# A decoder layer in f32: the FFN input's weight sums go to VectorE, and the FFN output's loads and the gate product to GpSimd

## The chip, the cores and the metric

The kernel runs on one core of a Trainium2 chip. The time is the device time of one execution in microseconds, as the median of several runs. TensorE (PE) multiplies matrices, VectorE (DVE) and ScalarE (ACT) work element by element and read PSUM, GpSimd (POOL) works element by element on SBUF only, and SyncE (SP) issues DMAs. ACT and POOL can issue DMAs too. Each engine takes its instructions in order.

## The reference

One layer of 1024 tokens and width 1024 in f32. Its last third is what the change touches:

```python
def conv_glu(hn, w_ffn_in, conv_w, conv_b, w_ffn_out):
    a, gate = jnp.split(hn @ w_ffn_in, 2, axis=-1)        # 1024 x 5632, D_FF = 2816
    a_pad = jnp.pad(a, ((0, 0), (CONV_W - 1, 0), (0, 0)))
    conv = conv_b + sum(a_pad[:, j:j + S] * conv_w[j] for j in range(CONV_W))
    return (jax.nn.gelu(conv) * gate) @ w_ffn_out          # 2816 x 1024
```

Ahead of it stand a mixer of sparse and differential attention and a cross attention over 256 memory tokens, which the change does not touch.

## The kernel before, in words

Every f32 operand of a large product is split into a high and a low half, each in f32r: ScalarE copies the high half (`parts`, line 175), VectorE subtracts it from the source for the low half (line 178). A product is then three matmuls for each 128 rows of the contraction (`mm3`, lines 281 to 283). A split pair of weights of 128x512 is a page (`wp`, 12 of them).

The FFN input is computed in 22 tiles of 128 features (`ffn_in(f)`), each with seven products of 512 columns in place of eight, after Strassen and Winograd: sums of the four quarters of the operands are multiplied, and sums of the products give the four quarters of the result. The activations' sums are made once. The weights' sums are made for every tile: the tile's weights arrive in two raw tiles of 128x2x512, `a` and `g` (line 162, 512 KB each, on SP's queue), and four jobs work on them. Job A splits `a`'s two halves, B makes three sums (lines 199 to 201) and splits two of them, C makes a fourth sum (line 207) and splits two more operands, D splits the last. In tile 0 these sums run on VectorE, in the others on GpSimd. There are two raw tiles (`NRAW`), and `W.pump` splits the next job as soon as pages are counted free.

Each product has a PSUM bank; six banks turn. An add on VectorE (line 1427) or a copy on ScalarE (line 1432) takes it out into `p1`, `u2`, `v5` and the result's halves `a` and `g`. Behind the last add the tile's tail runs: ScalarE takes the first tap of the convolution (line 1468, ident), VectorE the other two (lines 1469, 1470), ScalarE the GELU (line 1471), VectorE multiplies by the gate (line 1472), and the result goes to `u_d` in HBM from ScalarE's queue (line 1473). The buffers of `a`, `g` and the convolution come from four `kq` tiles.

The FFN output has seven products as well, and its operands' sums are made ahead, in between: after each tile `fo_sums` takes a pair of rows of `w_ffn_out` (side w) or of `u_d` (side u), loads four tiles `fs` of 128x512 (line 1515, SP's queue, four buffers), and owes four steps, each a sum on GpSimd (line 1518) and its store to `ws_d` or `us_d` from GpSimd's queue (line 1519). `sums_step` makes one owed step where it is called. Then the FFN output itself runs: 77 steps, each with two loads of 256 KB on SP's queue (lines 1547, 1548), 14 steps ahead, a split over 128x1024 (lines 1556, 1557), and four products.

Up to the end of tile 0 TensorE's order is that of the program; all other orders, on every engine, are set by a planner that simulates the program and takes, on each engine, the first instruction in the program's order that its simulated time has ready. The order is then fixed.

The lines that the steps turn on:

```python
self.nsplit += 1
if len(self.raws) < NRAW - 1 or self.nload < self.nsplit:
    self.load()
```

Of the kernel before, what the change touches and what calls it, by code (L numbers as in the profile page):

```python
# [9 lines left out]
F32 = mybir.dt.float32  # L10
# [8 lines left out]
P = 128  # L19
# [5 lines left out]
FT = 22  # L25
# [19 lines left out]
def hybrid_layer(ctx, tc, I, out):  # L45
# [15 lines left out]
    def nm(s):  # L61
        cnt[0] += 1
        return f"{s}_{cnt[0]}"
# [68 lines left out]
    def wp():  # L132
        return wpool.tile([P, 2, 512], F32R, name=nm("wp"), tag="wp", bufs=NWP)

    def rawt():
        return wpool.tile([P, 2, 512], F32, name=nm("raw"), tag="raw", bufs=NRAW)

    class Weights:
# [41 lines left out]
        def split(self):  # L180
# [9 lines left out]
            if kind == "A":  # L190
                fi["a"] = raw
                fpart(raw[:, 0, :])
                fpart(raw[:, 1, :])
            elif kind == "B":
                fi["g"] = raw
                fi["s"] = s1 = page_s()
                a, g = fi["a"], raw
                eng = dve if key == ("fi", 0) else pool
                eng.tensor_tensor(s1, g[:, 0, :], g[:, 1, :], op=OP.add)  # L199
                eng.tensor_tensor(g[:, 0, :], a[:, 0, :], g[:, 0, :], op=OP.subtract)  # L200
                eng.tensor_tensor(a[:, 0, :], s1, a[:, 0, :], op=OP.subtract)  # L201
                fpart(a[:, 0, :])
                fpart(s1)
            elif kind == "C":
                a, g = fi["a"], fi["g"]
                eng = dve if key == ("fi", 0) else pool
                eng.tensor_tensor(a[:, 1, :], a[:, 1, :], a[:, 0, :], op=OP.subtract)
                fpart(g[:, 0, :])
                fpart(a[:, 1, :])
            elif kind == "D":  # L210
                fpart(fi["g"][:, 1, :])
            elif kind == "memT":
                for j in range(2):
                    pg = self.page(key)
                    for b in range(2):
                        v = slice(256 * b, 256 * b + 256)
                        gk = gmem[:, n + 2 * j + b:n + 2 * j + b + 1]
                        act.activation(pg[:, 0, v], raw[:, j, v], AF.Copy, scale=gk)
                        dve.scalar_tensor_tensor(pg[:, 1, v], raw[:, j, v], gk, pg[:, 0, v].bitcast(F32),
                                                 op0=OP.mult, op1=OP.subtract)  # L220
            elif kind == "xq":
                for j in range(2):
                    pg, gk = self.page(key), gxa[:, engines + j:engines + j + 1]
                    pool.tensor_scalar(pg[:, 0, :], raw[:, j, :], gk, 1.0, op0=OP.mult, op1=OP.mult)
                    dve.scalar_tensor_tensor(pg[:, 1, :], raw[:, j, :], gk, pg[:, 0, :].bitcast(F32), op0=OP.mult, op1=OP.subtract)
            else:
                for j in range(2):
                    self.parts(self.page(key), raw[:, j, :n], n, engines[j])
            self.nsplit += 1
            if len(self.raws) < NRAW - 1 or self.nload < self.nsplit:  # L230
                self.load()

        def pump(self, n=1):
# [923 lines left out]
        return w2_at[0].tile(shape, dt, name=nm(name), tag="w2", bufs=w2_at[1])  # L1157

    def fs():
        return w2_at[0].tile([P, 512], F32, name=nm("fs"), tag="fs", bufs=4)  # L1160

    def page_s():
        return pgp.tile([P, 512], F32, name=nm("ws"), tag="ws", bufs=1)
# [257 lines left out]
    def ffn_in(f):  # L1421
# [47 lines left out]
        dve.scalar_tensor_tensor(cv[:, 1:], a[:, :T - 1], cw[:, f, 1:2], cv[:, 1:], op0=OP.mult, op1=OP.add)  # L1469
        dve.scalar_tensor_tensor(cv[:, 2:], a[:, :T - 2], cw[:, f, 0:1], cv[:, 2:], op0=OP.mult, op1=OP.add)  # L1470
        act.activation(cv, cv, AF.Gelu_apprx_tanh)
        dve.tensor_tensor(g, cv, g, op=OP.mult)
        act.dma_start(u_d[f * P:(f + 1) * P, :], g)
        sums_step(4)
        if f % 2:
            owed_sums.extend(fo_sums("w", f // 2))
        elif f:
            owed_sums.extend(fo_sums("u", f // 2 - 1))
        if f == FT - 1:
            sums_step(4)  # L1480
            owed_sums.extend(fo_sums("u", f // 2))
            sums_step(4)

# [22 lines left out]
    def fo_sums(side, m):  # L1508

        src, d = (u_src, us_d) if side == "u" else (w_src, ws_d)  # L1510
        x = {}
        for odd in range(2):
            for half in range(2):
                x[odd, half] = fs()
                sp.dma_start(x[odd, half], src(m, odd, half))

        def one(j, o, p, q, op=OP.subtract):
            pool.tensor_tensor(o, p, q, op=op)  # L1518
            pool.dma_start(sum_at(d, j, m), o)
        x11, x21 = x[0, 0], (x[0, 1] if side == "u" else x[1, 0])  # L1520
        x12, x22 = (x[1, 0] if side == "u" else x[0, 1]), x[1, 1]
        if side == "u":
            return [lambda: one(0, x22, x21, x22, OP.add), lambda: one(2, x21, x11, x21),
                    lambda: one(1, x11, x22, x11), lambda: one(3, x12, x12, x11)]
        return [lambda: one(0, x11, x12, x11), lambda: one(2, x12, x22, x12),
                lambda: one(1, x22, x22, x11), lambda: one(3, x21, x21, x22)]

    owed_sums = []

# [43 lines left out]
            pass  # L1573

    w2_st.close()
    w2_at[:] = [ctx.enter_context(tc.tile_pool(name="w2q", bufs=1, reuse_waits="tile")), 5]
    for f in range(1, FT):
        for _ in ffn_in(f):
            pass
# [112 lines left out]
```

## Time and profile before

| what | value |
|---|---|
| median of 3 runs | 1758.92 us (1758.91 to 1760.85) |
| the profiled execution | 1757.62 us, span 1755.8 us |
| granted TensorE clock, mean | 0.957 |
| busy, PE / PEld / DVE / ACT / POOL | 91% / 74% / 73% / 42% / 38% |
| chain that ended last, by engine | PE 40%, DVE 31%, DMA 11%, issue 9%, POOL 5% |
| DMA | 220 MB, mean 125 GB/s |

A line of the page's groups reads: line, engine, operation, output<-input, count, then the busy time and the mean of one in ns, then the engine's idle time just before them and what ended it. Idle time is what an engine spends between instructions; a wait within an instruction shows as a longer duration. The granted clock is a share of 2.4 GHz; a stretch at 0.50 ran at 1.2 GHz.

### The profile page before, as it was taken

Reading aid. Unit: us, or ns where it says so; the run is one execution under the profiler, and the core shown is the slowest. Engines: PE = TensorE matmul, PEld = TensorE weight load, DVE = VectorE, ACT = ScalarE, POOL = GpSimd, SP = SyncE. Lnnn points to the kernel's source line nnn. Section 1 sums busy time; section 2 is a strip of 40 time slices with the busy share of each in tenths; the row PEclk is TensorE's granted clock in tenths of the full one; section 3 lists DMA queues with packets and bytes.
Section 4 is the critical chain, followed back from the end, with each engine's and each line's share of the span. In section 5 each row is a group of like instructions: output and inputs, shape, how many; then the busy total and the mean of one; then the engine's idle time right before and its main releaser. Section 6 shows DMA issues by size and latency. Waiting matters only on the chain.

```text
span 1755.8 us, 22643 instructions
## 1 busy us (share of the span) xinstructions
PE 1597.7 (91%) x7660; PEld 1303.6 (74%) x7660; DVE 1281.3 (73%) x2461; ACT 739.5 (42%) x1469; POOL 674.9 (38%) x862
## 2 busy tenths in 40 slices
PE   8899898788889999999999979998889889889999
PEld 7788676677777779877777757776667667668887
DVE  5746999998999894476453897777777777645564
ACT  6545576665664236144431343322222222333442
POOL 1647567356310230221010165654556655330111
PEclk9999989898999999999999989999999999889999
DMA  8222135222121221443030214444444444698811
GB/s 279 87 85 65 56 99 167 71 91 75 56 82 49 84 73 43 128 149 107 1 109 35 93 44 165 158 160 162 168 156 155 146 144 162 237 361 311 288 49 66
DMA packets 117795, 220.07 MB, mean 125 GB/s; under 512 B 18480, under 2 KB 38448, under 8 KB 117680
## 3 DMA queue, kind: packets, MB, share of 16 engines
q1 hardware_dynamic: 103744, 171.44, 29.8%
q0 software_dynamic: 8320, 27.27, 4.0%
q10 hardware_dynamic: 5616, 19.93, 2.9%
q8 instruction: 60, 0.98, 0.2%
q14 instruction: 55, 0.45, 0.1%
HBM read 160.92 MB, written 57.67 MB: 124 GB/s over the span
## 4 chain that ended last, share of the span: by engine, by line
PE 40%; DVE 31%; DMA 11%; issue 9%; POOL 5%; ACT 3%; SPq 0%; POOLq 0%; DVEq 0%; ACTq 0%
PE acc L281 7%; PE acc L282 7%; PE acc L283 7%; DVE jk L538 5%; DVE wp L178 5%; DMA raw<-in_w_ffn_in_dram 5%; PE big L281 2%; PE big L283 2%; PE big L282 2%; PE big L1249 2%; POOL raw L201 2%; DVE fc L1470 2%; PE acc L1010 1%; DVE ea L992 1%; DVE e L747 1%
## 5 line engine op out<-in xcount | busy, mean ns | idle before, releaser
L178 DVE TENSOR_TENSOR wp<-raw,wp 128x512 fp32r<-128x512 f32 (+1 forms) x200 | 214.4, 1087 | 97.6 <-ACT wp L175 89.7
L175 ACT CAST wp<-raw 128x512 fp32r<-128x512 f32 (+1 forms) x188 | 111.2, 616 | 221.9 <-DMA raw<-in_w_ffn_in_dram 94.3
L1557 DVE TENSOR_TENSOR wp<-fo,wp 128x1024 fp32r<-128x1024 f32 x77 | 99.9, 1312 | 95.5 <-ACT wp L1556 92.1
L1518 POOL TENSOR_TENSOR fs<-fs,fs 128x512 f32<-128x512 f32 x88 | 125.7, 1429 | 68.3 <-DMA fs<-in_w_ffn_out_dram 56.8
L1556 ACT CAST wp<-fo 128x1024 fp32r<-128x1024 f32 x77 | 79.7, 1049 | 128.3 <-PE big L283 47.3
L281 PE MATMUL acc<-wp,xh 128*128 128x512 f32 (+1 forms) x272 | 111.0, 411 | 8.7 <-ACT X L619 8.7
L177 POOL TENSOR_SCALAR wp<-raw 128x512 fp32r<-128x512 f32 (+1 forms) x64 | 45.3, 718 | 180.1 <-DVE rst L110 63.5
L282 PE MATMUL acc<-wp,xh 128*128 128x512 f32 (+1 forms) x272 | 110.4, 407 | 0.0
L283 PE MATMUL acc<-wp,xl 128*128 128x512 f32 (+1 forms) x272 | 110.2, 406 | 0.0
L655 ACT COPY pt<-trp 128x512 f32<-128x512 f32 (+3 forms) x144 | 65.6, 476 | 73.4 <-PE trp L664 72.9
L178 POOL TENSOR_TENSOR wp<-raw,wp 128x512 fp32r<-128x512 f32 x52 | 69.2, 1348 | 46.1 <-ACT wp L175 45.9
L199 POOL TENSOR_TENSOR ws<-raw 128x512 f32<-128x512 f32 x21 | 29.4, 1400 | 146.2 <-DMA raw<-in_w_ffn_in_dram 95.2
L1602 POOL TENSOR_TENSOR hr<-hr,r 128x512 f32<-128x512 f32 x16 | 26.8, 1688 | 152.1 <-DVE r L1618 78.6
L1010 PEld LDWEIGHTS acc<-va_t,pt 128*128 128x128 f32 x576 | 73.4, 193 | 6.4 <-ACT pt L655 4.3
L1010 PE MATMUL acc<-va_t,pt 128*128 128x65 f32 x576 | 75.8, 271 | 2.2 <-ACT pt L655 1.9
L1055 POOL DMA_DIRECT2D h_d<-xr x16 | 9.4, 586 | 167.0 <-DVE xr L1054 148.7
L993 ACT ACTIVATE ea<-ea,sta 128x128 f32<-128x128 f32 (+7 forms) x64 | 49.4, 777 | 51.4 <-DVE sta L992 47.9
L281 PEld LDWEIGHTS acc<-wp,xh 128*128 128x128 f32 x272 | 53.2, 196 | 21.9 <-ACT X L619 10.5
L538 DVE TENSOR_SCALAR_CACHE_REDUCE jk<-mb,cx 128x640 bf16<-128x640 uint16 (+1 forms) x64 | 68.6, 1072 | 0.7
L538 DVE TENSOR_SCALAR_CACHE_REDUCE jk<-mb,cand 128x640 bf16<-128x640 bf16 (+3 forms) x60 | 64.4, 1074 | 0.4
L282 PE MATMUL acc<-wp,wp 128*128 128x512 f32 x152 | 61.4, 404 | 3.5 <-DVE wp L178 3.0
L1469 DVE SCALAR_TENSOR_TENSOR fc<-fa,cw,fc 128x1023 f32<-128x1023 f32 x22 | 42.6, 1937 | 27.5 <-ACT fc L1468 27.5
(419 smaller groups left out, 5168.9 us busy)
## 6 DMA issues: line engine op xcount, KB each, us to landing
raw<-in_w_ffn_in_dram SPq DMA_DIRECT2D x44, 512.0 KB, 5.1
fs<-in_w_ffn_out_dram SPq DMA_DIRECT2D x44, 256.0 KB, 4.8
u_d<-fg ACTq DMA_DIRECT2D x22, 512.0 KB, 5.2
ws_d<-fs POOLq DMA_DIRECT2D x44, 256.0 KB, 2.7
fs<-u_d SPq DMA_DIRECT2D x44, 256.0 KB, 3.3
us_d<-fs POOLq DMA_DIRECT2D x44, 256.0 KB, 2.3
fo<-us_d SPq DMA_DIRECT2D x44, 256.0 KB, 5.3
fo<-ws_d SPq DMA_DIRECT2D x44, 256.0 KB, 5.4
```

Of the source, the lines that this page charges most:

```text
L175: act.copy(pg[:, 0, :n], src)
L178: (dve if el == "d" else pool).tensor_tensor(pg[:, 1, :n], src, pg[:, 0, :n].bitcast(F32), op=OP.subtract)
L281: pe.matmul(o, lhsT=lh, rhs=rh, start=start, stop=False)
L282: pe.matmul(o, lhsT=lh, rhs=rl, start=False, stop=False)
L283: pe.matmul(o, lhsT=ll, rhs=rh, start=False, stop=stop)
L538: dve.tensor_scalar(jk[:, :n], src, th[:, j:j + 1], None, op0=OP.is_ge, op1=OP.add, accum_out=cnt[:, j:j + 1])
L655: act.copy(dst, src)
L993: last["act"] = act.activation(e[:, :n], e[:, :n], AF.Exp, bias=st[:, 0, h:h + 1], scale=-1.0)
L1010: pe.matmul(acc[:, hh * 65:hh * 65 + 65], lhsT=pt, rhs=va_t[:, kt, :], start=kt == 0, stop=kt == i)
L1518: pool.tensor_tensor(o, p, q, op=op)
L1556: act.copy(hi, raw)
L1557: dve.tensor_tensor(lo, raw, hi.bitcast(F32), op=OP.subtract)
```

## The change

Seven things change. The four sums of a tile's weights run on VectorE in all tiles; the first three are made in job A, which now loads `g` itself if it is not there, the fourth in job B. From tile 1 on there is a third raw tile, taken by every third load, and loads run one further ahead. `w2` has four buffers in that stage instead of five, and `fs` three instead of four. The gate product and the store to `u_d` go to GpSimd and its queue, except in the last tile. The loads of `fo_sums` go to GpSimd's queue. They are no longer issued together when the sums become owed: a first owed step issues three, and the fourth follows the third sum, so five steps are owed for each side. `sums_step` is called once more in each tile, and with 5 instead of 4 at its end.

```diff
+    raw3 = []
     def rawt():
+        if raw3:
+            raw3[1] += 1
+            if raw3[1] % 3 == 0:
+                return raw3[0].tile([P, 2, 512], F32, name=nm("raw"), tag="raw3", bufs=1)
         return wpool.tile([P, 2, 512], F32, name=nm("raw"), tag="raw", bufs=NRAW)
...
             if kind == "A":
                 fi["a"] = raw
                 fpart(raw[:, 0, :])
                 fpart(raw[:, 1, :])
+                if i + 1 not in self.raws:
+                    self.load()
+                a, g = raw, self.raws[i + 1]
+                fi["s"] = s1 = page_s()
+                dve.tensor_tensor(s1, g[:, 0, :], g[:, 1, :], op=OP.add)
+                dve.tensor_tensor(g[:, 0, :], a[:, 0, :], g[:, 0, :], op=OP.subtract)
+                dve.tensor_tensor(a[:, 0, :], s1, a[:, 0, :], op=OP.subtract)
             elif kind == "B":
                 fi["g"] = raw
-                fi["s"] = s1 = page_s()
-                a, g = fi["a"], raw
-                eng = dve if key == ("fi", 0) else pool
-                eng.tensor_tensor(s1, g[:, 0, :], g[:, 1, :], op=OP.add)
-                eng.tensor_tensor(g[:, 0, :], a[:, 0, :], g[:, 0, :], op=OP.subtract)
-                eng.tensor_tensor(a[:, 0, :], s1, a[:, 0, :], op=OP.subtract)
+                a = fi["a"]
                 fpart(a[:, 0, :])
-                fpart(s1)
+                fpart(fi["s"])
+                dve.tensor_tensor(a[:, 1, :], a[:, 1, :], a[:, 0, :], op=OP.subtract)
             elif kind == "C":
-                a, g = fi["a"], fi["g"]
-                eng = dve if key == ("fi", 0) else pool
-                eng.tensor_tensor(a[:, 1, :], a[:, 1, :], a[:, 0, :], op=OP.subtract)
-                fpart(g[:, 0, :])
-                fpart(a[:, 1, :])
+                fpart(fi["g"][:, 0, :])
+                fpart(fi["a"][:, 1, :])
...
-            if len(self.raws) < NRAW - 1 or self.nload < self.nsplit:
+            if len(self.raws) < NRAW - 1 + len(raw3) // 2 or self.nload < self.nsplit:
...
-        return w2_at[0].tile([P, 512], F32, name=nm("fs"), tag="fs", bufs=4)
+        return w2_at[0].tile([P, 512], F32, name=nm("fs"), tag="fs", bufs=3)
...
-        dve.tensor_tensor(g, cv, g, op=OP.mult)
-        act.dma_start(u_d[f * P:(f + 1) * P, :], g)
-        sums_step(4)
+        if f == FT - 1:
+            dve.tensor_tensor(g, cv, g, op=OP.mult)
+            act.dma_start(u_d[f * P:(f + 1) * P, :], g)
+        else:
+            pool.tensor_tensor(g, cv, g, op=OP.mult)
+            pool.dma_start(u_d[f * P:(f + 1) * P, :], g)
+        sums_step(5)
...
-        x = {}
-        for odd in range(2):
-            for half in range(2):
-                x[odd, half] = fs()
-                sp.dma_start(x[odd, half], src(m, odd, half))
+        def ld(odd, half):
+            t = fs()
+            pool.dma_start(t, src(m, odd, half))
+            return t
...
+            def start():
+                x["22"], x["21"], x["11"] = ld(1, 1), ld(0, 1), ld(0, 0)
+
+            def third():
+                one(1, x["11"], x["22"], x["11"])
+                x["12"] = ld(1, 0)
+            return [start, lambda: one(0, x["22"], x["21"], x["22"], OP.add), lambda: one(2, x["21"], x["11"], x["21"]),
+                    third, lambda: one(3, x["12"], x["12"], x["11"])]
...
-    w2_at[:] = [ctx.enter_context(tc.tile_pool(name="w2q", bufs=1, reuse_waits="tile")), 5]
+    w2_at[:] = [ctx.enter_context(tc.tile_pool(name="w2q", bufs=1, reuse_waits="tile")), 4]
+    raw3[:] = [w2_at[0], 0]
```

Side w of `fo_sums` is changed in the same way as side u, shown here.

## Rows read from the trace of the kernel before

**Rows 1.** The page: busy us (share of the span) xinstructions of each engine.

```profile
PE 1597.7 (91%) x7660; PEld 1303.6 (74%) x7660; DVE 1281.3 (73%) x2461; ACT 739.5 (42%) x1469; POOL 674.9 (38%) x862
```

**Rows 2.** Windows: length, busy us (instructions) by engine, granted clock, DMA share, GB/s.

```profile
1083.00:1524.00 441.00, 394.54 (x1597) 311.02 (x1596) 326.37 (x311) 123.60 (x183) 254.38 (x226) 0.95 0.46 156
1524.00:1570.00 46.00, 33.81 (x125) 26.25 (x124) 24.45 (x25) 17.09 (x18) 6.91 (x7) 0.81 1.01 375
1570.00:1752.00 182.00, 181.81 (x803) 150.20 (x801) 98.77 (x90) 67.78 (x69) 34.28 (x24) 1.00 0.53 189
```

**Rows 3.** TensorE's timeline: start us, duration us, line, operation, output<-input, idle and releaser.

```profile
1290.80 0.40 PE L281 MATMUL acc<-B,wp 128*128 128x512 f32 x1
...
1293.60 0.40 PE L281 MATMUL trp<-T,wp 128*128 128x512 f32 x1
...
1330.38 0.76 PE L281 MATMUL acc<-B,wp 128*128 128x512 f32 x1 [3.83 <-DVE fg L1427]
```

**Rows 4.** TensorE's waits, 1083 to 1524: us in total, times, longest; six rows.

```profile
PE trp L281 <- DVE fg L1427: 12.7, 3, 4.3
...
PE big L281 <- DVE u L1427: 1.4, 1, 1.4
```

**Rows 5.** Window right behind a long wait of TensorE.

```profile
1330.00:1335.00 5.00, 4.62 (x11) 3.68 (x12) 5.00 (x6) 1.57 (x2) 1.79 (x2) 0.50 0.45 161
```

**Rows 6.** Chain of waits, 1311 to 1337: start us, us, what.

```profile
1312.86 5.02 DMA raw<-in_w_ffn_in_dram
...
1324.27 0.63 ACT wp L175
...
1329.56 0.68 DVE fg L1427
...
1332.98 1.22 DVE wp L178 x2
...
1334.22 4.79 DMA raw<-in_w_ffn_in_dram
```

**Rows 7.** VectorE's timeline in that stretch.

```profile
1324.92 4.71 DVE L178 TENSOR_TENSOR wp<-raw,wp 128x512 fp32r<-128x512 f32 x1 [1.84 <-ACT wp L175]
```

**Rows 8.** GpSimd's timeline in that stretch.

```profile
1324.76 1.31 POOL L1518 TENSOR_TENSOR fs<-fs,fs 128x512 f32<-128x512 f32 x1
...
1327.80 1.27 POOL L1518 TENSOR_TENSOR fs<-fs,fs 128x512 f32<-128x512 f32 x1
1329.37 0.56 POOL L1519 DMA_DIRECT2D us_d<-fs  x1 [0.30 <-POOL fs L1518]
```

**Rows 9.** VectorE by line, 1083 to 1524: count, busy us, mean ns, idle before, releaser.

```profile
L178 DVE TENSOR_TENSOR wp<-raw,wp 128x512 fp32r<-128x512 f32 x106 | 138.8, 1322 | 78.1 <-ACT wp L175 78.1
L1469 DVE SCALAR_TENSOR_TENSOR fc<-fa,cw,fc 128x1023 f32<-128x1023 f32 x19 | 37.9, 1993 | 26.1 <-ACT fc L1468 26.1
```

**Rows 10.** SP's queue's waits, 1083 to 1524.

```profile
SPq L162 <- DVE wp L178: 107.5, 34, 7.0
SPq L1515 <- POOL fs L1518: 107.1, 19, 10.7
```

**Rows 11.** Window of the instructions on raw tiles: VectorE, ScalarE, GpSimd busy.

```profile
1083.00:1524.00 441.00, 138.81 (x106) 63.29 (x106) 105.58 (x72) 0.95 0.46 156
```

**Rows 12.** GpSimd by line, whole span: a 128x1024 tensor_tensor.

```profile
L1174 POOL TENSOR_TENSOR kxl<-kxr,kxh 128x1024 fp32r<-128x1024 f32 x2 | 4.8, 2403 | 0.2
```

**Rows 13.** DMA issues, 1083 to 1524: count, size, median us to landing.

```profile
fs<-in_w_ffn_out_dram SPq DMA_DIRECT2D x38, 256.0 KB, 4.3
u_d<-fg ACTq DMA_DIRECT2D x19, 512.0 KB, 5.2
```

**Rows 14.** GpSimd's DMA issues to us_d: ns min/median/max.

```profile
L1519 POOL DMA_DIRECT2D us_d<-fs x40: 557/557/559, 1089.6 to 1517.5; - x40
```

**Rows 15.** TensorE's waits, 1524 to the end.

```profile
PE acc L281 <- ACT wp L1556: 7.4, 1, 7.4
PE acc L281 <- DVE v L1427: 4.2, 1, 4.2
```

More of the change, by code (lines that the diff above doesn't have):

```diff
@@ L1478, in ffn_in @@
             owed_sums.extend(fo_sums("u", f // 2 - 1))
+        sums_step()
         if f == FT - 1:
-            sums_step(4)
+            sums_step(5)
             owed_sums.extend(fo_sums("u", f // 2))
-            sums_step(4)
+            sums_step(5)
     NM = FT // 2
@@ L1519, in one, with start, third @@
             pool.dma_start(sum_at(d, j, m), o)
-        x11, x21 = x[0, 0], (x[0, 1] if side == "u" else x[1, 0])
-        x12, x22 = (x[1, 0] if side == "u" else x[0, 1]), x[1, 1]
+        x = {}
         if side == "u":
[L1523 to L1526, printed above, removed]
+            def start():
[5 more added lines that the diff above has]
+                    third, lambda: one(3, x["12"], x["12"], x["11"])]
+        def start():
+            x["11"], x["12"], x["22"] = ld(0, 0), ld(0, 1), ld(1, 1)
+        def third():
+            one(1, x["22"], x["22"], x["11"])
+            x["21"] = ld(1, 0)
+        return [start, lambda: one(0, x["11"], x["12"], x["11"]), lambda: one(2, x["12"], x["22"], x["12"]),
+                third, lambda: one(3, x["21"], x["21"], x["22"])]
     owed_sums = []
```

## The prediction

> **What bounds the kernel now.** I read the page's busy shares first: TensorE is busy 91% of a span of 1755.8 us and no other engine over 73% [rows 1], so the question is where TensorE is not at full speed. The table of windows answers it by stage [rows 2]: the FFN input's steady part, 1083 to 1524 us, has TensorE busy 394.5 of 441 us at a granted clock of 0.95; the change of stage behind it, 46 us, only 33.8 at 0.81; and the FFN output that follows is full (181.8 of 182, clock 1.00). Nothing is to be won in the last.
>
> In the timeline of TensorE a product of 12 matmuls takes 2.80 us when it is fed (one begins at 1290.80, the next at 1293.60) [rows 3]. The 441 us hold 1596 matmuls, 19 tiles of 84, which at that pace is 133 x 2.80 = 372.4 us. So 68.6 us are lost, and a tile takes 23.2 us where 19.6 would do. TensorE's waits in the window stand in six rows from 12.7 down to 1.4 us, 46.3 us together [rows 4]. The other 22 us follow each long wait: behind the one that ends at 1330.38 the window 1330 to 1335 has a granted clock of 0.50, the 1.2 GHz level, against 1.00 in the FFN output [rows 2, 3, 5]. What removes a wait gives its 2 us or so of slow clock back too.
>
> All these waits name an add on VectorE (line 1427), which frees the PSUM bank that the product wants. The add is late, not slow (0.68 us). The chain of waits shows why, from 1312.86 on [rows 6]: a raw weight tile is loaded (5.02 us), GpSimd makes its sums (landed 1317.9, done 1324.2, with a sum of the FFN output between them), ScalarE makes the high half (0.63 at 1324.27), and then VectorE's low half starts at 1324.92 and lasts 4.71 us [rows 7], where a free operation of its shape, as the add, takes 0.68. The add of `fg` stands behind it, at 1329.56, and TensorE goes on at 1330.38. In GpSimd's timeline three tensor_tensors and a DMA issue fill those 4.1 us without a pause [rows 8]; VectorE gets in at the first gap, at 1329.07. The same picture (one split of about 4.7 us behind such a run) stands in most tiles: the 106 splits of this form average 1322 ns [rows 9]. Then the other splits free the raw tile, and only at 1334.22 does the next load start. With two raw tiles for two loads a tile, this ring (load, sums, splits, free) is the period: 21.4 us here, and SP's queue spends 107.5 us waiting for a split to free a raw tile [rows 10].
>
> **The change part by part.**
> *Sums to VectorE, at the job before.* GpSimd loses 4 tensor_tensors a tile, 72 in the window and 105.6 us [rows 11], 5.9 us a tile. VectorE gets them: no row shows this sum there, the nearest is the split (same shape, two inputs in SBUF): two of them begun within 1.22 us when nothing holds them [rows 6], 1.32 each on average as they are held now. I take 0.60, so 2.4 us a tile, the upper end being 5.3. In the ring the sums' 6.2 us become about 2.
>
> *Third raw tile.* The first load of a tile no longer waits for the tile before. The ring now spans three half-tile slots: load 5.0, sums 1.8, five casts (0.62) and splits (0.60) and 2 us of waits, so some 15 us, against the 29 us (1.5 x 19.6) that three slots allow. The load is then hidden; if it weren't, the 5 us would be back. The price in SBUF (one `w2` and one `fs` buffer less) I put at nothing: three `w2` tiles live per product tile, four remain, and the FFN output's residual tiles come four at a time.
>
> *Gate product to GpSimd.* VectorE loses a 128x1024 tensor_tensor (1.2 us, twice the 0.60). GpSimd gains one; the row of that shape there takes 2.40 us [rows 12]. It lies at the end of a tile's chain (ident, convolution, GELU, gate, store). Its result's buffer is wanted only when the next tile's convolution buffer is taken, one tile later. Counted from the last add: ident, two of convolution and GELU at no more than the 2.0 us that the slowest of them has on average [rows 9], 8 us, then 2.4 + 0.6 for gate and issue and a store of 5.2 [rows 13]: 16.2 us, under 19.6. Hidden as long as GpSimd gets to it within 3 us.
>
> *Loads to GpSimd's queue.* Four loads and the store of u are issued there, 0.557 us each [rows 14], 2.8 us a tile; SP loses the loads, which held it 107.1 us and more [rows 10]. Raw loads, and later the FFN output's, stand free behind them. GpSimd per tile: 4 x 1.30 + 2.40 + 9 x 0.557 + 4 pauses of 0.30 = 13.8 us, plus what it waits for loads.
>
> The Trainium skill (SBUF — State Buffer, Summary: rules for kernel authors) advises against DMAs from GpSimd beside VectorE, since descriptor generation is starved while VectorE runs a two-port mode. The 40 issues from there to us_d last 557 to 559 ns with VectorE busy 74% of the time [rows 2, 14], so nothing of it shows. If it held for these operations, the five new issues would each wait for one operation of 0.7 to 2 us.
>
> *VectorE's own time*, the new limit to look at: 7 splits, 7 adds at 0.60 and three passes of 1.2 are 12.0 us now; 12.0 + 2.4 - 1.2 = 13.2 after. It is busy 326.4 / 19 = 17.2 us a tile now [rows 2], so 5 to 6 us are waits behind GpSimd. GpSimd's reading operations fall from 8 x 1.3 = 10.4 to 5.2 + 2.4 = 7.6 us, and its sums now alternate with their own stores, with a pause after each, so the runs of 4 us go. In proportion 4.3 us of waits are left: 17.5, with the 1.4 us in which the convolution waits for ScalarE [rows 9] 18.9 of 19.6. That fits, barely. The same page (section "Who interferes with whom") has the loser wait for one instruction of the other; the row of 4.71 us shows a wait over three. By the page the wait would be smaller than mine.
>
> I therefore don't take TensorE's floor but a period of 20.7 us, 1.1 above it: about the share that the waits now have, scaled by GpSimd's smaller part, (23.2 - 19.6) x 4.3 / 5.5 x 0.4, where 0.4 is my estimate of how much of a wait still reaches TensorE once sums and load are off the ring. The gain is (23.2 - 20.7) x 19 = 48 us.
>
> *The change of stage.* TensorE waits 4.2 us for an add and 7.4 us for a cast there [rows 15]. The first loads of the FFN output stand in SP's queue behind fs loads, though the first of them needs only the pages that the last tile's first product frees, some 13 us before the tile's end; with SP free it can go earlier. The bounds are -14 us (both waits and their slow clock go) and +5 (one more landing exposed, as the 5.2 us of the store of u [rows 13]); I take -3, since the 7.4 us hang on the last tile's store, which stays on ScalarE's queue.
>
> Sum: the profiled execution took 1757.6 us; 1757.6 - 48 - 3 = 1706.6, and the median of the runs is 1.3 above it: 1708.
>
> **Rivals.**
> *GpSimd becomes the period.* It runs in order, and its loads now wait where its arithmetic is queued. If each tile is gate, store, three loads, three sums, load, sum, one after the other, both load times are exposed: 13.8 + 2 x 4.3 (the median landing of the loads of w [rows 13]) = 22.4 us. A late gate then holds the convolution buffer, ScalarE's in-order queue and its casts. Gain (23.2 - 22.4) x 19 = 15: about 1743. For it: one buffer fewer for these loads, and none is fetched ahead. Against: the second load's wait can be filled by the next gate. The skill's starvation rule would add five waits of 0.7, 3.5 us, and turn this into a loss.
>
> *VectorE becomes the period (slower).* If GpSimd's reads block it for their whole length, 13.2 + 7.6 + 1.4, and it still waits for casts as now (78.1 / 19 = 4.1 [rows 9]), a tile takes 26.3 us: 3.1 x 19 = 59 us more, about 1817. It decides from the point at which VectorE's waits pass 10.0 us a tile (13.2 + 10.0 = 23.2). The likelier small form is the sums themselves: they stand in VectorE's order ahead of adds and wait there for the load; with a whole load of 5.0 us exposed in each tile, VectorE's 18.9 become 23.9, 0.7 over the old period: 1772. Against: the second load of a tile starts when the fifth split is done, well ahead.
>
> *The stall only moves (no change).* The order of instructions is set by the planner's own clock; if splits still stand ahead of late operands, the period stays: 1759.
>
> **How the numbers follow.** Forecast (period 19.6 to about 21.9, and the bounds of the change of stage; 1676 to 1730): 0.57. GpSimd as period (1730 to 1755): 0.19. No change: 0.08. Slower: 0.16, mostly its small form. A difference under 0.2% (3.5 us) can't be told from none. Faster 0.76, same 0.08, slower 0.16. Most of the forecast's mass lies above the floor; the range is 1682 to 1754, which takes in the GpSimd case; the forecast's own range is 1682 to 1728.
>
> **What would show it.** Right: the splits' mean under 0.9 us, none of 4.7; GpSimd without lines 199 to 207; raw loads issued with no wait of a whole tile; TensorE's waits in the stage under 20 us and its clock at 0.98 or more. GpSimd's rival: gates that start 5 us or more after GELU ends, ScalarE waiting for the store of u. VectorE's: sums waiting for raw loads, VectorE busy over 90%. A prediction of 1708 is wrong if the tile's period stays above 22 us, or if the change of stage costs 5 us or more.

## The result, and the profile after

The changed kernel takes 1694.44 us (median of 4 runs, 1689.76 to 1697.69) against 1759.88 for the kernel before on the same chip: a ratio of 0.963, 95% interval 0.960 to 0.965. Predicted were 1708 us, in a range of 1682 to 1754. The profiled execution took 1697.69 us; all stage figures below are of profiled executions.

The page of the changed kernel: span, and busy us of each engine as in [rows 1].

```profile
span 1695.9 us, 22395 instructions
...
PE 1570.8 (93%) x7660; PEld 1284.2 (76%) x7660; DVE 1296.0 (76%) x2524; ACT 736.7 (43%) x1469; POOL 666.8 (39%) x908
```

TensorE has 27 us less busy time for the same 7660 matmuls: its clock was slow for less of the time. Windows of the changed kernel, columns as in [rows 2]. The first is the same 19 tiles (1596 matmuls, counted back from the FFN input's last one), the second the change of stage, the third the FFN output.

```profile
1081.89:1472.88 390.99, 376.98 (x1597) 298.49 (x1596) 343.07 (x370) 124.00 (x185) 241.60 (x260) 1.00 0.53 180
1472.88:1510.00 37.12, 30.26 (x124) 24.49 (x123) 18.88 (x14) 12.34 (x13) 18.20 (x20) 0.91 0.91 335
1510.00:1692.00 182.00, 181.84 (x803) 150.23 (x801) 97.34 (x90) 67.83 (x69) 38.87 (x30) 1.00 0.58 209
```

Counted the same way the stage before was 441.05 us, and what follows it to the end of the span 231.69; now they are 390.99 and 223.02 (1695.9 - 1472.88). So of the 59.9 us by which the span is shorter, 50.1 come from the stage (a period of 20.58 us instead of 23.21), 8.7 from behind it and 1.2 from ahead of it. The granted clock of the stage rose from 0.95 to 1.00.

TensorE's waits in the stage (us in total, times, longest), which answer to [rows 4]; three smaller rows between the third and the last are left out:

```profile
PE acc L287 <- DVE fa L1433: 3.9, 4, 1.5
PE big L287 <- DVE fa L1433: 3.7, 4, 1.4
PE trp L287 <- DVE fa L1433: 3.4, 3, 1.8
...
PE trp L287 <- DVE v L1433: 0.6, 1, 0.6
```

All seven rows together are 14.0 us where there were 46.3, and the longest wait is 1.8 us where it was 5.3. They still name VectorE's adds. VectorE's lines in the stage, as in [rows 9]: the high-low splits, both convolution passes, and the first of the weight sums that it now makes (count, busy us, mean ns, idle before and its releaser).

```profile
L184 DVE TENSOR_TENSOR wp<-raw,wp 128x512 fp32r<-128x512 f32 x106 | 118.2, 1115 | 4.9 <-ACT wp L181 4.9
L1476 DVE SCALAR_TENSOR_TENSOR fc<-fa,cw,fc 128x1022 f32<-128x1022 f32 x19 | 47.1, 2481 | 0.0
L1475 DVE SCALAR_TENSOR_TENSOR fc<-fa,cw,fc 128x1023 f32<-128x1023 f32 x19 | 31.7, 1668 | 12.6 <-ACT fc L1474 12.6
L204 DVE TENSOR_TENSOR ws<-raw 128x512 f32<-128x512 f32 x17 | 17.4, 1022 | 27.4 <-DMA raw<-in_w_ffn_in_dram 27.4
```

The second convolution pass had this line before the change:

```profile
L1470 DVE SCALAR_TENSOR_TENSOR fc<-fa,cw,fc 128x1022 f32<-128x1022 f32 x19 | 29.3, 1542 | 0.0
```

The splits fell from 1322 to 1115 ns, but that pass (now L1476) went from 1542 ns to 2481: VectorE is still held, by other instructions and at other places. Its timeline in one tile (start, duration, line), the two held ones:

```profile
1321.54 2.81 DVE L1476 SCALAR_TENSOR_TENSOR fc<-fa,cw,fc 128x1022 f32<-128x1022 f32 x1
...
1326.05 2.51 DVE L184 TENSOR_TENSOR wp<-raw,wp 128x512 fp32r<-128x512 f32 x1 [0.49 <-ACT wp L181]
```

and GpSimd's timeline beside it:

```profile
1321.95 1.31 POOL L1529 TENSOR_TENSOR fs<-fs,fs 128x512 f32<-128x512 f32 x1
...
1325.59 2.41 POOL L1482 TENSOR_TENSOR fg<-fc,fg 128x1024 f32<-128x1024 f32 x1 [0.93 <-ACT fc L1477]
1328.44 1.28 POOL L1529 TENSOR_TENSOR fs<-fs,fs 128x512 f32<-128x512 f32 x1 [0.43 <-DMA fs<-in_w_ffn_out_dram]
```

The pass overlaps one operand sum; the split starts half a us into the gate's product, which ends at 1328.00, and lasts until 1328.56: nearly the whole of a free split (0.68 us) comes behind the gate. Splits of 4.7 us beside runs of three GpSimd operations [rows 7, 8] are gone, the longest of the stage lasts 3.3 us; single operations, sums and the gate, still hold VectorE.

SP's queue in the stage, as in [rows 10]:

```profile
SPq L168 <- DVE wp L184: 340.7, 33, 20.1
```

Its wait for a free raw tile grew from 107.5 to 340.7 us. That is no new stall: until the FFN output's first loads the queue has nothing else to issue, stands ready, and waits for a free raw tile as it should.

Behind the stage TensorE has one wait, which takes the place of both in [rows 15]:

```profile
PE acc L287 <- DVE fg L1433: 6.9, 1, 6.9
```

How it comes about is read from three timelines around it: GpSimd,

```profile
1477.04 0.55 POOL L1525 DMA_DIRECT2D fs<-u_d  x1 [0.81 <-DMA us_d<-fs]
1479.24 0.55 POOL L1525 DMA_DIRECT2D fs<-in_w_ffn_out_dram  x1 [1.64 <-DMA us_d<-fs]
1479.80 2.35 POOL L1482 TENSOR_TENSOR fg<-fc,fg 128x1024 f32<-128x1024 f32 x1
```

ScalarE, with the GELU whose result that gate takes,

```profile
1461.85 1.06 ACT L1477 ACTIVATE fc<-fc 128x1024 f32<-128x1024 f32 x1 [2.73 <-DVE fc L1476]
...
1482.19 1.24 ACT L1474 ACTIVATE fc<-fa,cw 128x1024 f32<-128x1024 f32 x1 [9.78 <-POOL fg L1482]
```

and VectorE.

```profile
1483.46 1.95 DVE L1475 SCALAR_TENSOR_TENSOR fc<-fa,cw,fc 128x1023 f32<-128x1023 f32 x1 [10.83 <-ACT fc L1474]
1485.33 0.68 DVE L1433 TENSOR_TENSOR fg<-acc,u 128x512 f32<-128x512 f32 x1
```

The gate of the last tile but one stands on GpSimd behind loads that wait for earlier stores to land. It starts at 1479.80, 16.9 us after its GELU ended, and holds the convolution buffer: ScalarE's first pass of the last tile waits 9.78 us for it, VectorE 10.83 us for ScalarE, and the add behind, which frees TensorE's bank, starts only at 1485.33.

### The profile page after: what moved, and what is told of

Same layout as the page of the kernel before. It is cut to its first block, busy times and chain, and to the rows that moved or that the text cites. A ratio compares the mean times of both kernels' runs of the same rounds, so it can differ in the third digit from the quotient of the medians.

```text
span 1695.9 us, 22395 instructions
## 1 busy us (share of the span) xinstructions
PE 1570.8 (93%) x7660; PEld 1284.2 (76%) x7660; DVE 1296.0 (76%) x2524; ACT 736.7 (43%) x1469; POOL 666.8 (39%) x908
## 4 chain that ended last, share of the span: by engine, by line
PE 47%; DVE 31%; DMA 8%; issue 6%; POOL 5%; ACT 3%; SPq 0%; ACTq 0%; DVEq 0%; POOLq 0%
PE acc L287 8%; PE acc L288 8%; PE acc L289 8%; DVE jk L544 6%; DVE wp L184 4%; PE big L288 3%; PE big L287 3%; PE big L289 3%; DMA fs<-u_d 2%; POOL fs L1529 2%; PE trp L287 2%; PE trp L288 2%; PE trp L289 2%; PE big L1255 2%; DMA raw<-in_w_ffn_in_dram 2%
## 5 line engine op out<-in xcount | busy, mean ns | idle before, releaser
L184 DVE TENSOR_TENSOR wp<-raw,wp 128x512 fp32r<-128x512 f32 (+1 forms) x200 | 192.9, 973 | 21.8 <-ACT wp L181 13.2
L1580 DVE TENSOR_TENSOR wp<-fo,wp 128x1024 fp32r<-128x1024 f32 x77 | 100.6, 1322 | 76.8 <-ACT wp L1579 75.2
L1482 POOL TENSOR_TENSOR fg<-fc,fg 128x1024 f32<-128x1024 f32 x21 | 50.9, 2425 | 36.3 <-ACT fc L1477 36.1
L1474 ACT ACTIVATE fc<-fa,cw 128x1024 f32<-128x1024 f32 x22 | 27.4, 1245 | 81.9 <-DVE fa L1433 72.2
```

Source lines behind the costliest of these rows:

```text
L184: (dve if el == "d" else pool).tensor_tensor(pg[:, 1, :n], src, pg[:, 0, :n].bitcast(F32), op=OP.subtract)
L1482: pool.tensor_tensor(g, cv, g, op=OP.mult)
L1580: dve.tensor_tensor(lo, raw, hi.bitcast(F32), op=OP.subtract)
```

## The experiments

Twelve kernels were run, named by what they take out of the changed kernel, or add to it or to the kernel before. "Stage" is the 19 tiles, "rest" what lies between them and the end of the span; TensorE alone needs 372.4 us (19.60 a tile) in the stage. The runs whose names begin with e1 to e5, g and h1 start from the changed kernel and keep its five steps of `fo_sums`, its three `fs` and its four `w2` buffers; h2, h3 and e6 start from the kernel before. What loads on SP's queue cost in e4, e5 and g3 is therefore measured with three `fs` buffers, not with the four of before.

| run | sums on VectorE | third raw | loads on GpSimd | gate on GpSimd | stage (period), us | rest, us | median, us | ratio to before |
|---|---|---|---|---|---|---|---|---|
| before | no | no | no | no | 441.05 (23.21) | 231.69 | 1759.88 | |
| after | yes | yes | yes | yes | 390.99 (20.58) | 223.02 | 1694.44 | 0.963 [0.960, 0.965] |
| e1_no_third_raw | yes | no | yes | yes | 399.6 (21.03) | 215.0 | 1702.09 | 0.969 [0.966, 0.972] |
| e2_sums_gpsimd | no | yes | yes | yes | 407.3 (21.44) | 262.8 | 1758.07 | 1.000 [0.998, 1.002] |
| e3_gate_vector | yes | yes | yes | no | 372.40 (19.60) | 224.1 | 1684.77 | 0.958 [0.956, 0.960] |
| e4_loads_sync | yes | yes | no | yes | 393.6 (20.72) | 233.0 | 1713.13 | 0.974 [0.971, 0.977] |
| e5_sums_raw_only | yes | yes | no | no | 391.5 (20.60) | 231.8 | 1708.24 | 0.972 [0.970, 0.974] |
| g2_gate_vector_no_third_raw | yes | no | yes | no | 411.1 (21.63) | 224.5 | 1725.22 | 0.981 [0.979, 0.983] |
| g3_sums_only | yes | no | no | no | 408.7 (21.51) | 232.4 | 1731.55 | 0.985 [0.983, 0.988] |
| g1_last_store_gpsimd | yes | yes | yes | no | 372.4 (19.60) | 214.2 | 1674.03 | 0.953 [0.951, 0.954] |
| h1_sums_at_b | yes | yes | yes | no | 372.4 (19.60) | 214.1 | 1675.10 | 0.951 [0.949, 0.953] |
| h2_before_last_store_gpsimd | no | no | no | no | 443.4 (23.34) | 221.9 | 1746.78 | 0.993 [0.992, 0.995] |
| h3_before_fo_sums_vector | no | no | no | no | 387.5 (20.40) | 231.8 | 1705.60 | 0.969 [0.967, 0.970] |
| e6_before_no_fo_sums | no | no | no | no | 372.4 (19.60) | 223.2 | 1677.79 | 0.955 [0.952, 0.957] |

**e1_no_third_raw.** The changed kernel with two raw tiles again.

```diff
-    raw3[:] = [w2_at[0], 0]
```

> The changed kernel with two raw tiles in all tiles. Theory 'ring': load, sums, splits and the freeing of a raw tile bounded the tile before; with the sums on VectorE the ring is 4.3 (load) + 2.5 (sums) + 8 (casts, splits, waits), about 15 us of the 19.6 that two slots allow, but the second load now starts only behind the last split of the tile before, and the sums stand in VectorE's queue ahead of adds and wait there. I expect 0.5 to 1.2 us more a tile: 1705 to 1720 us, with VectorE's waits for raw loads at over 60 us in the stage (27 with three). Rival 'port' (only the splits that GpSimd held up counted, the third raw tile is idle luxury): 1690 to 1698 us, waits for raw loads as with three.

Measured: 1702 us, stage +8.6 us. VectorE's first sum waits 37.5 us for raw tiles instead of 27.4. The time lies between the ranges of the theory and the rival, with shorter waits for raw tiles than the theory had (over 60 us). The third tile is worth little here; with the gate on VectorE it is worth 38.7 us (g2 against e3, below). (The rest is shorter by 8.0: in this run the gate of the last tile but one starts 10.9 us after its GELU instead of 16.9, and costs TensorE 1.3 us instead of 6.9.)

**e2_sums_gpsimd.** The weight sums back on GpSimd, at jobs B and C; the other three parts stay. The edit is shortened here; job A loses its sums.

```diff
 B: fi["g"] = raw
+   fi["s"] = s1 = page_s()
+   pool.tensor_tensor(s1, ...), pool.tensor_tensor(g, ...), pool.tensor_tensor(a, ...)
 C:
+   pool.tensor_tensor(a[:, 1, :], a[:, 1, :], a[:, 0, :], op=OP.subtract)
```

> The changed kernel with the four weight sums back on GpSimd in jobs B and C, third raw tile, gate and loads as changed. 'Ring': three slots carry a longer ring, so the load stays hidden, but GpSimd has 13.8 + 5.9 = 19.7 us of work a tile beside its waits for loads (3 to 5 us): a period of 22.5 to 24 us, 1725 to 1760 us, GpSimd busy over 80% in the stage. 'Port': the long splits of over 4 us are back, and VectorE's splits average over 1.2 us; the same time. Rival 'raw tile alone' (the third tile is what gave the gain): 1690 to 1705 us.

Measured: 1758 us, no gain left. The time lies in the expected range and the splits average 1420 ns as expected, but the period does not fit: 21.44 us where 22.5 to 24 were expected. The stage is still 33.8 us shorter than before, but GpSimd doesn't get its work done in it. The waits behind the stage say where that comes due:

```profile
ACT wp L1579 <- DMA fo<-us_d: 63.5, 3, 29.5
...
PE acc L287 <- ACT wp L1579: 44.0, 2, 25.3
```

The FFN output's casts wait 63.5 us for operand sums that GpSimd has not yet stored, and TensorE 44.0 us for the casts. With the weight sums on it, GpSimd has no room for the gate and the loads.

**e3_gate_vector.** The gate's product on VectorE and its store on ScalarE's queue for every tile, as before the change.

```diff
-        if f == FT - 1:
+        if True:
             dve.tensor_tensor(g, cv, g, op=OP.mult)
             act.dma_start(u_d[f * P:(f + 1) * P, :], g)
```

> The changed kernel with the gate product on VectorE and its store on ScalarE's queue in all tiles. VectorE has 1.2 us more a tile of its own, GpSimd 2.4 + 0.57 less. If VectorE's time is what sets the 20.9 us, the period grows by about 0.5 to 1.2 us in spite of less contention: 1700 to 1715 us. If GpSimd's reads that hold VectorE up (the second convolution pass averages 2.48 us) set it, the period falls to 20.0 to 20.6: 1675 to 1690 us. In both the wait of 6.9 us at the change of stage goes, since the gate of tile 20 no longer waits in GpSimd's queue (minus 7 us, in these numbers).

Measured: 1685 us, faster than the full change, with a period below either theory's. The stage is at TensorE's floor; its window, and VectorE's lines in it:

```profile
1086.42:1458.82 372.40, 372.40 (x1597) 298.45 (x1596) 322.55 (x387) 132.04 (x186) 190.70 (x229) 1.00 0.56 192
```

```profile
L184 DVE TENSOR_TENSOR wp<-raw,wp 128x512 fp32r<-128x512 f32 x105 | 81.4, 775 | 0.0
...
L1476 DVE SCALAR_TENSOR_TENSOR fc<-fa,cw,fc 128x1022 f32<-128x1022 f32 x19 | 29.2, 1536 | 0.0
L1479 DVE TENSOR_TENSOR fg<-fc,fg 128x1024 f32<-128x1024 f32 x19 | 28.0, 1475 | 12.0 <-ACT fc L1477 12.0
```

VectorE gets 28.0 us of gates and is yet busy 20.5 us less (322.55 against 343.07). So its other instructions took 48.5 us less, 2.55 a tile: with the gate and its store on GpSimd, VectorE was spared 1.5 us a tile and lost 2.55. This is near the 2.41 us that the gate lasts on GpSimd, but the gate's own hold is less. In the changed kernel's trace one VectorE instruction lasts 2.5 to 3.3 us beside 12 of the stage's 18 gates, and beside five VectorE runs nothing. An estimate, from each VectorE instruction's time above the usual shortest of its form, put to the GpSimd operation beside it: some 22 us were lost beside gates, and 67 beside operand sums, where e3 loses 48. So about half of the charge comes from the gate itself, the other half from sums that VectorE's instructions meet more often; why they do was not followed.

The expected 7 us at the change of stage did not come: the rest is 224.1 us, no shorter than in the changed kernel (223.0). The 6.9 us are gone, but a wait for a cast stands in their place:

```profile
PE acc L287 <- ACT wp L1579: 6.2, 1, 6.2
```

**e4_loads_sync.** The operand sums' loads back on SP's queue.

```diff
-            pool.dma_start(t, src(m, odd, half))
+            sp.dma_start(t, src(m, odd, half))
```

> The changed kernel with the loads of the FFN output's operand sums back on SP's queue, in the new five steps with three buffers. Theory: they stand in front of raw loads and of the FFN output's first loads and hold SP until their buffers are free. Raw loads then come late in the stage (VectorE waits for them over 60 us, 27 now), and the FFN output's first load goes less than 12 us before the last product's end (24 now): 1715 to 1740 us, some 10 of it at the change of stage. Rival (SP's waits were idle time that cost nothing, and GpSimd's queue is the worse place): 1685 to 1695 us.

Measured: 1713 us. In the stage it is only 2.6 us, behind it 10.0: the FFN output's first loads stand behind those on SP. VectorE waits 35.3 us for raw tiles (27.4 in the changed kernel), less than the 60 expected, and the time is 2 us below the expected range.

**g1_last_store_gpsimd.** e3 with the last tile's store of u issued from GpSimd instead of ScalarE.

```diff
-            act.dma_start(u_d[f * P:(f + 1) * P, :], g)
+            (pool if f == FT - 1 else act).dma_start(u_d[f * P:(f + 1) * P, :], g)
```

> The kernel with the gate product on VectorE (e3), with the last tile's store of u issued by GpSimd instead of ScalarE. In e3 that store's issue stands 12.7 us in ScalarE's queue behind its finished operand (1467.3 to 1480.0), the casts of the FFN output behind it, and TensorE waits 6.2 us. Theory: the issue waits for something of the hardware-issued DMAs in flight, so on GpSimd's queue ScalarE goes on at once: 8 us less than e3, 1674 to 1679 us, no wait of TensorE for a cast over 1 us. Rival (the casts wait for their loads, the bus is full at that point): 1683 to 1687 us, ScalarE's wait then shown for DMA fo at the same place.

What it takes away is seen in e3, ScalarE's timeline behind the last GELU, which began at 1465.06:

```profile
1480.02 0.33 ACTq L1480 DMA_DIRECT2D u_d<-fg  x1
1480.46 5.78 ACT L1579 CAST wp<-fo 128x1024 fp32r<-128x1024 f32 x6 [14.34 <-DMA fo<-in_w_ffn_out_dram]
```

The gate on VectorE is done at 1467.39, the store is issued 12.6 us later, and six casts of the FFN output stand behind it in ScalarE's order. The trace puts the casts' wait down to a load of `fo`; but six of them run without a pause as soon as the store is issued, so their operands were there. The trace's semaphores say what held it. The instruction ahead of the issue waits for the semaphore that the store will itself signal, and loads of `fo` on SP's queue signal the same one; the last of these was issued at 1474.55 and landed at 1479.94. In the kernel before such a load lands at 1553.59 and the store is issued at 1553.67, in e5 at 1506.26 and 1506.34. In the changed kernel the two times are 1491.40 and 1491.75, but there the last gate itself was done only at 1490.76. The store from GpSimd, in g1:

```profile
1467.71 0.54 POOL L1480 DMA_DIRECT2D u_d<-fg  x1 [4.13 <-DVE fg L1479]
```

ScalarE's timeline of g1 has the casts right behind the GELU,

```profile
1466.06 2.93 ACT L1579 CAST wp<-fo 128x1024 fp32r<-128x1024 f32 x3
```

and the window of its change of stage has TensorE busy for the whole of it at full clock:

```profile
1458.11:1500.00 41.89, 41.89 (x186) 34.70 (x185) 28.46 (x20) 19.70 (x21) 17.30 (x19) 1.00 1.05 393
```

Measured: 1674 us, the fastest of these kernels; the rest falls by 9.9 us to 214.2, and TensorE waits for no cast. The expectation held.

**g2_gate_vector_no_third_raw** is e3 with e1's edit; **g3_sums_only** leaves, of the change, the weight sums on VectorE a job ahead, and the five steps and fewer buffers of `fo_sums` (e3's, e4's and e1's edits on the changed kernel).

> The kernel with the gate product on VectorE (e3), with two raw tiles. e3's stage ran at TensorE's floor, 19.60 us a tile. Theory: with the gate off GpSimd, VectorE has slack, and the second slot's load (4.3 us) fits: period 19.6 to 19.9, 1683 to 1692 us; the third raw tile then only hid what the gate on GpSimd cost. Rival ('ring' still binds without it, as in e1 by 0.45 us a tile): period 20.1 or more, 1692 to 1700 us.

> Of the change only the sums on VectorE a job ahead: gate on VectorE and its store from ScalarE, loads of the FFN output's operands on SP's queue (in the new five steps, three buffers), two raw tiles. Theory (GpSimd's sums in the ring and the runs that hold VectorE's splits are the loss): most of the gain is there, period 19.8 to 20.8, and the change of stage keeps the cost of SP's queue: 1695 to 1715 us. Rival (the parts need each other: raw loads behind the waiting loads on SP are late, and with two raw tiles nothing hides it): period over 21.5, 1725 us or more.

Measured: 1725 and 1732 us. Both miss what the theory gave them; g3 fits its rival, g2 lies above its rival's range too. With two raw tiles the stage does not come to the floor though the gate is on VectorE: 21.63 and 21.51 us a tile. A part of the reason stands at VectorE's first sum; g2:

```profile
L204 DVE TENSOR_TENSOR ws<-raw 128x512 f32<-128x512 f32 x17 | 11.8, 692 | 47.4 <-DMA raw<-in_w_ffn_in_dram 47.4
```

VectorE stands 47.4 us before loads of raw tiles, with its adds queued behind. In e3 that is 19.5 us. The sums' place in VectorE's order has a price: the load's landing is exposed there, not on GpSimd. But the length of this wait alone does not decide: in e5, below, it is 45.0 us, and the stage is 19.6 us shorter than in g2.

Against e1, which differs only in the gate and its store, g2's stage is 11.5 us longer: with two raw tiles the gate is better on GpSimd. With loads on SP's queue its place is worth 2.1 us (e4 against e5). The 18.6 us of e3 belong to the third raw tile and the free queue as much as to the gate.

**e6_before_no_fo_sums.** The kernel before without GpSimd's operand sums; loads and stores stay. It leaves out work that the layer needs and serves for its times alone.

```diff
-            pool.tensor_tensor(o, p, q, op=op)
             pool.dma_start(sum_at(d, j, m), o)
```

> The kernel before, with the FFN output's operand sums left out (88 tensor_tensors on GpSimd; the loaded tiles are stored unsummed). GpSimd keeps the weights' four sums and all DMA issues. Theory 'port': the 4.7 us splits are those that wait behind a run of GpSimd's reads of two kinds; without the FFN output's sums a run is at most the weight sums, so the splits' mean falls from 1.32 to under 1.0 us, the ring to 17 to 19 us, and the period to 19.6 to 20.6: 1690 to 1715 us. Rival (the sums' own 5.9 us on GpSimd and the load in the ring are enough to bound it): period 22 or more, 1735 us or more.

Measured: 1678 us (two runs), better than either theory gave, with the period at the lower edge of the first. With two raw tiles and the weight sums on GpSimd the stage is at the floor, as its window shows,

```profile
1082.82:1455.22 372.40, 372.40 (x1597) 300.05 (x1596) 269.21 (x318) 126.92 (x187) 143.20 (x149) 1.00 0.58 195
```

and VectorE's splits in it, which answer to [rows 9], are short.

```profile
L178 DVE TENSOR_TENSOR wp<-raw,wp 128x512 fp32r<-128x512 f32 x106 | 83.3, 799 | 67.2 <-ACT wp L175 67.2
```

They take 799 ns instead of 1322. So the ring of two raw tiles was not by itself the limit; it was long with GpSimd's second stream of reads between the sums and beside the splits. One rival is not apart from this here: without the sums the `fs` buffers come free sooner, and SP's waits for them, behind which raw loads stand, fall from 272 us in the stage to 113.

**h1_sums_at_b.** g1 with the first three weight sums in job B, where their splits are, not a job ahead. The edit is shortened here.

```diff
-A: dve.tensor_tensor(s1, ...), dve.tensor_tensor(g, ...), dve.tensor_tensor(a, ...)
+B: dve.tensor_tensor(s1, ...), dve.tensor_tensor(g, ...), dve.tensor_tensor(a, ...)
```

> The fastest version so far (g1: changed kernel, gate on VectorE, last store of u from GpSimd), with the first three sums made in job B, where their results are split, instead of a job ahead. Theory: the third raw tile has both loads there in time, the planner puts the sums where it has their data anyway, and the stage stays at TensorE's floor: period 19.6 to 19.9, 1672 to 1682 us. Rival (a job ahead matters: the splits of B wait for sums that have just begun, and adds stand behind them): period 20.2 or more, 1685 us or more.

Measured: 1675 us against 1674 for g1: no difference. VectorE's 2545 instructions come out in the same order in both, so "a job ahead" changes nothing in this kernel.

**h2_before_last_store_gpsimd.** The kernel before with g1's edit alone.

> The kernel before, with the last tile's store of u issued by GpSimd and nothing else changed. Theory: before, too, that issue stood in ScalarE's queue (operand done 1541.2, issued 1553.67) and TensorE's 7.4 us behind it go: the stage unchanged at 441 us, the rest 222 to 225 us instead of 231.7: 1746 to 1752 us. Rival (the wait moves to the loads, or the new instruction shifts the planner's orders): 1753 us or more.

Measured: 1747 us; the rest falls by 9.8 us, as in g1, and TensorE's 7.4 us for the cast [rows 15] are gone while its wait for the add stays (4.8). The stage is 2.4 us longer.

**h3_before_fo_sums_vector.** The kernel before with the operand sums, not the weight sums, on VectorE: one word.

```diff
-            pool.tensor_tensor(o, p, q, op=op)
+            dve.tensor_tensor(o, p, q, op=op)
```

> The kernel before, with the FFN output's operand sums on VectorE instead of GpSimd (one word changed; the weights' sums stay on GpSimd, two raw tiles, loads on SP, gate on VectorE). Theory 'port': what cost the stage was two streams of reads on GpSimd, run together; taking either off is enough. GpSimd reads 5.2 us a tile instead of 10.4, VectorE has 2.4 us more of its own: period 19.6 to 20.8, 1685 to 1712 us. Rival (the weights' sums must leave GpSimd, because they stand in the ring of the raw tile): period 22 or more, 1735 us or more; or VectorE, with more work and waits for the loads of these sums in its order, gets worse.

Measured: 1706 us, as the theory of GpSimd's reads expected. Its stage:

```profile
1084.06:1471.58 387.52, 377.66 (x1597) 297.93 (x1595) 292.61 (x390) 120.37 (x182) 134.94 (x150) 1.00 0.53 178
```

20.40 us a tile without a third raw tile, without moved loads and with the weight sums where they were: VectorE is busy 33.8 us less than before [rows 2] although it makes 80 sums more. SP's queue still waits 185 us for `fs` buffers here, and VectorE's splits are as short as in e6 (788 ns), which speaks for GpSimd's reads as the larger part of the loss; what the shorter waits on SP's queue (272 us before) add to the gain no run takes apart.

**e5_sums_raw_only.** e3 with e4's edit: sums and third raw tile, loads on SP.

> Of the change the sums on VectorE and the third raw tile: gate on VectorE and its store from ScalarE, loads of the FFN output's operands on SP's queue in the new five steps. Theory: these two parts carry the stage, which stays at TensorE's floor (19.60 us a tile, 372 to 376 us, as in e3), and the loads' place only shows at the change of stage, which keeps about 232 us for the rest: 1690 to 1696 us. Rival (with loads waiting on SP ahead of raw loads, the third tile fills late): period over 20.3, 1700 us or more.

Measured: 1708 us; the rival was right and the theory not. The loads' place costs 19.1 us in the stage here, where it cost 2.6 with the gate on GpSimd. SP's queue from 1086 to 1460 us, most of the stage:

```profile
SPq L1525 <- DMA us_d<-fs: 138.4, 27, 9.2
SPq L168 <- DVE wp L184: 85.0, 24, 8.4
SPq L1525 <- POOL fs L1529: 56.7, 25, 6.0
```

The operand loads (L1525) wait there for their buffers, the raw loads stand behind them, and VectorE's first sum waits 45.0 us for raw tiles. Both the third tile and the loads' move serve to have a raw tile landed when VectorE comes to it: its wait is 19.5 us with both (e3) and 40 to 47 with one or none. Against g3's stage the third tile alone brings 17.2 us (e5), the loads' move alone none (g2, 2.4 us longer), both together 36.3.

## Why the prediction was right, and where it was not

*The stage: -48 predicted, -50.1 measured; period 20.7 against 20.58.* The mechanism held: VectorE's splits were late because GpSimd's reads held them; long runs went, a part of the waits stayed. TensorE's waits under 20 us (14.0), clock at 0.98 or more (1.00) and no split of 4.7 us (3.3 at most) came as named. Splits under 0.9 us did not (1115 ns): the gate holds them too. Raw loads "with no wait of a whole tile" did not either, as worded: SP's longest wait for a free raw tile is 20.1 us, though it no longer stands behind other loads. That the period came out within 0.12 us is in part luck: the 1.1 us above the floor were set by a factor of 0.4 that no row gave.

*What made up that number was not as told.* "Gate product to GpSimd ... Hidden" is the step that failed. The product was hidden from GpSimd's own schedule but not from VectorE: I booked 1.2 us saved on VectorE, and counted the 2.4 us only in a proportion (4.3 of 5.5 us of waits left). In e3 the whole leftover of 0.98 us a tile, 18.6 us, goes with the gate and its store; without them on GpSimd the period is TensorE's floor, which I had declined to forecast. It does so only beside the third raw tile and the free queue (g2, e5). The Trainium skill (SBUF — State Buffer, Summary: rules for kernel authors) has the second of two such instructions, one on VectorE with two SBUF inputs and one on GpSimd that reads SBUF, blocked until the first finishes. The split that began 0.46 us into a gate and ended 0.56 us behind it agrees; the one of 4.71 us across three operations [rows 7, 8] waited longer than that.

*The ring (load, sums, splits, free) as the period* was half right. e6 and h3 show two raw tiles to be enough for 19.60 and 20.40 us once the operand sums leave GpSimd. The ring's 21.4 us were in good part made of GpSimd's interleaved operations. With the sums on VectorE, though, the third tile does matter, for another reason than I gave: VectorE stands before the load (g2). One `w2` and one `fs` buffer less, which I put at nothing, cost the stage nothing in e3, which is at the floor with them.

*Sums on VectorE: 2.4 us a tile* is 3.3 (the four lines' 56.3 us over 17 tiles), inside the bound of 5.3; in e3 2.9.

*The change of stage: -3 predicted, -8.7 measured*, between the bounds of -14 and +5. The term was mis-sized. Loads off SP give 8 to 10 us there in three pairs (after against e4, g2 against g3, e3 against e5), and the wait for the add goes with them. The wait for the cast hung on the last tile's store, as I said: issued from GpSimd, it takes that wait away in g1 and h2, for 9.9 and 9.8 us. But that they would stay with the store on ScalarE's queue was wrong: in the changed kernel it is issued 1.0 us after its gate, and no cast is waited for. The late gate took 6.9 us back; in e1, where it costs 1.3, the rest is 215.0.

*The rivals.* "GpSimd becomes the period" did not happen in the steady tiles, and happened once, as it was worded: at the last tile but one, a gate 16.9 us behind its GELU that held the convolution buffer, ScalarE and TensorE. "VectorE becomes the period", small form (sums waiting for raw loads), is what g2, g3 and e5 show, at 45 to 47 us in g2 and e5 and not as a loss against before. "The stall only moves" fell.

*Left open.* The median of the changed kernel lies 3.3 us below its profiled execution; where the faster executions save that was not traced. Why the late gate came later in the changed kernel than in e1 was not tried. No run takes SP's waits for `fs` buffers out of the kernel before while GpSimd keeps both kinds of sums, so how much of its loss was the queue's stays open.

## What to carry to other kernels

When an elementwise operation with two SBUF inputs is moved from VectorE to GpSimd, count what it may take from VectorE beside what it spares: here 1.5 us a tile spared and 2.55 lost. Moving work the other way can make VectorE less busy (h3: 80 more operations, 33.8 us less). Whether the time follows depends on what else binds: the gate's way back gained 18.6 us in e3, 2.1 with loads on SP's queue, and lost 11.5 with two raw tiles. An operation that must wait for a load delays what is queued behind it; on the critical engine the load has to be early, which here took a further buffer and a free queue together. A DMA issue on an engine that also computes can hold up that engine's next stage: look at when it is issued, not only when its operand is done, and at which other queue's DMAs signal its semaphore.

## What was not expected of the hardware

- A split of 0.68 us lasts 4.71 us across three GpSimd sums in a row [rows 7, 8], with a DMA issue but no pause between them, and 2.51 us across one gate. Both end 0.56 us after GpSimd's arithmetic has stopped, at 1329.63 and 1328.56; the first did not get in after the first of the three sums. Two lines of GpSimd's timeline before, which stand between the first two of [rows 8]:

```profile
1326.01 1.27 POOL L207 TENSOR_TENSOR raw<-raw 128x512 f32<-128x512 f32 x1
1327.22 0.56 POOL L1519 DMA_DIRECT2D us_d<-fs  x1
```

- One store on ScalarE's queue was issued 12.6 us after its operand was done, 0.08 us after a load on SP's queue landed that signals the same semaphore; from GpSimd's queue it was issued 0.3 us after its operand.
- GpSimd's DMA issues take 551 to 566 ns on average in the changed stage with VectorE busy 88% of it (343.07 of 390.99), against 557 at 74% before [rows 14]; with five more of them a tile, none of it shows as a longer issue.
- Waits of TensorE of up to 1.8 us left the granted clock of the stage at 1.00; behind the 3.83 us of [rows 3] it was 0.50 [rows 5].
